# A column sum over 32768 rows: another cut of the last rows, fewer passes on the tensor engine and one sum on GpSimd

## The chip, the cores and the metric

The kernel runs on one core of a Trainium2 chip. The time is in device microseconds for one execution. A core has five engines that run side by side, each with its own queue of instructions: TensorE (PE in the profile), VectorE (DVE), ScalarE (ACT), GpSimd (POOL) and SyncE (SP), which here only starts transfers. Transfers are carried out by 16 DMA engines. Engines wait for each other and for transfers through semaphores. SBUF is the on-chip memory of 128 partitions; TensorE writes its results to PSUM, a second and smaller memory.

## The reference

The input `grad_output` has the shape 32 x 1024 x 2048 in float32, 268 MB. The result is its sum over the first two axes, 2048 numbers:

```python
def reference(grad_output):
    return np.sum(grad_output, axis=(0, 1)).astype(np.float32)
```

## The kernel before

The input is read as 32768 rows of D = 2048 columns. A *row* below means 128 of these, one on each of the 128 partitions: 1 MB, and there are 256. Everything lies in three buffers of SBUF, `ring[0]` to `ring[2]`, each with room for M = 8 rows. `load(s, at, m)` (line 53) starts one transfer on SP's queue, which brings the next m rows into buffer s from place `at` on. `plus(s, to, n, s2, of)` (line 60) is one VectorE instruction, which adds n rows of buffer s2 to n rows of buffer s. `fold(s, m, left)` (line 64) halves m rows by such sums until `left` remain. All of them run in the order in which they are written, each engine's in its own queue; a wait is set only where one needs what another engine wrote or where a place is still being read.

**The chain** (lines 90 to 99) takes 29 loads of 8 rows. Of each load the first four rows take up the running four rows of the buffer before, and then the last four rows are added: two sums of 4 x 2048 columns for 8 rows. At the end four rows of a running sum stand in the last buffer, here called `run`.

**The end** (lines 102 to 143) covers the remaining 24 rows. They come as 8 rows in `s8`, 7 in `s7`, 3 in `run` at places 4 to 6, 3 in `run` at places 1 to 3, and three last rows that come singly, each cut in two: the first C = 1792 columns and, after all three, the last B = 256 columns (`LATE`). VectorE folds `run`'s four running rows to one (place 0), `s8`'s eight to one, `s7`'s seven to two, and adds `run`'s place 5 to its place 4. The three last rows go to places of `s8` that its sums no longer need: places 1 to 3, and 4 for the 256-column ends. SP's queue holds the loads in the order of the program, so a load that waits holds up those behind it.

**TensorE** adds up the partitions. `sums(s, at)` (line 76), called a row pass here, multiplies a column of ones with one row. It has four matmuls, each of a quarter of the columns, which work beside each other in four column groups of the array and add their results into partitions 0, 32, 64 and 96 of `acc` in PSUM. A float32 matmul stands in the profile as two records, so a pass has 8 records of matmuls and 8 of weight loads. There are twelve passes in a fixed order: `run` 6, `run` 0, `s8` 0, `s7` 0, `s7` 1, `run` 1, 2, 3, `s8` 1, `s8` 2, `run` 4, `s8` 3 (the number is the place in the buffer). After these come six small matmuls for the 256-column ends, into `accr`.

**The result** (lines 147 to 161): ScalarE copies `acc` to SBUF (`res`); ScalarE and GpSimd copy 384 columns each into `joint`; VectorE adds `accr`; three transfers write the 2048 numbers out. GpSimd's copy (line 150) is all that it computes in this kernel.

Of the kernel before, what the change touches and what calls it, by code (L numbers as in the profile page):

```python
# [1 line left out]

# [4 lines left out]

P = 128
M = 8
SLOTS = 3  # L10
CHAIN = 29
B = 256
LATE = 3


@with_exitstack
def kernel(
    ctx: ExitStack,
    tc: tile.TileContext,
    grad_output: bass.AP,  # L20
    out: bass.AP,
):

    nc = tc.nc
    f32 = mybir.dt.float32
    D = out.shape[-1]
    flat = grad_output.rearrange("b s d -> (b s) d")
    Q = D // 4
    H = B // 2
    C = D - B
    add = mybir.AluOpType.add

    sb = ctx.enter_context(tc.tile_pool(name="sb", bufs=1))
    ps = ctx.enter_context(tc.tile_pool(name="ps", bufs=1, space=bass.MemoryType.PSUM))
    ring = [sb.tile([P, M * D], f32, name=f"ring{s}") for s in range(SLOTS)]
    ones = sb.tile([P, 1], f32, name="ones")
    res = sb.tile([P, Q], f32, name="res")
    joint = sb.tile([P, C - 2 * Q], f32, name="joint")
    acc = ps.tile([P, 512], f32, name="acc")
    accr = ps.tile([P, 512], f32, name="accr")
    q, v, t, a, p = nc.sync, nc.vector, nc.tensor, nc.scalar, nc.gpsimd

    row = 0

    def load(s, at, m):

        nonlocal row
        src = flat[row * P : (row + m) * P].rearrange("(p m) d -> p (m d)", p=P)
        q.dma_start(out=ring[s][:, at * D : (at + m) * D], in_=src)
        row += m

    def plus(s, to, n, s2, of):  # L60
        part = ring[s][:, to * D : (to + n) * D]
        v.tensor_tensor(out=part, in0=part, in1=ring[s2][:, of * D : (of + n) * D], op=add)  # L62

    def fold(s, m, left):
        while m > left:
            n = m // 2
            plus(s, 0, n, s, m - n)
            m -= n

    def shares(x):  # L70


        ends = x[:, 2 * Q :].rearrange("p (b g c) -> p g b c", g=2, c=H)
        return [x[:, :Q], x[:, Q : 2 * Q], ends[:, 0], ends[:, 1]]

    def sums(s, at, w=D):
        for g, x in enumerate(shares(ring[s][:, at * D : at * D + w])):
            o = acc[32 * g : 32 * g + 1, : Q if g < 2 else (w - 2 * Q) // 2]
            t.matmul(  # L79
                o if g < 2 else o.rearrange("p (b c) -> p b c", c=H),  # L80
                lhsT=ones[:],
                rhs=x,
                start=False,
                stop=False,
                tile_position=(0, 32 * g),
                skip_group_check=True,
            )

    with tc.manual_schedule():
        for i in range(CHAIN):  # L90
            s = i % SLOTS
            load(s, 0, M)
            if i == 0:
                v.memset(ones[:], 1.0)  # L94
                v.memset(acc[:], 0.0)  # L95
                v.memset(accr[:], 0.0)  # L96
            else:
                plus(s, 0, 4, (i - 1) % SLOTS, 0)
            plus(s, 0, 4, s, 4)


        run, s8, s7 = (s, *((s + k) % SLOTS for k in (1, 2)))
        load(s8, 0, 8)
        fold(run, 4, 1)
        load(s7, 0, 7)
        fold(s8, 8, 1)
        load(run, 4, 3)
        fold(s7, 7, 2)
        plus(run, 4, 1, run, 5)
        load(run, 1, 3)  # L110
        tail = flat[row * P :]
        for k in range(3):
            q.dma_start(
                out=ring[s8][:, (1 + k) * D : (1 + k) * D + C], in_=tail[k * P : (k + 1) * P, :C]
            )
        for k in range(LATE):
            q.dma_start(
                out=ring[s8][:, 4 * D + k * B : 4 * D + (k + 1) * B],
                in_=tail[k * P : (k + 1) * P, C:],
            )  # L120
        sums(run, 6)
        sums(run, 0)
        sums(s8, 0)
        sums(s7, 0)
        sums(s7, 1)
        for at in (1, 2, 3):
            sums(run, at)
        sums(s8, 1, C)
        sums(s8, 2, C)
        sums(run, 4)  # L130
        sums(s8, 3, C)
        for k in range(LATE):
            for g in (2, 3):
                x = 4 * D + k * B + (g - 2) * H
                t.matmul(  # L135
                    accr[32 * g : 32 * g + 1, :H],
                    lhsT=ones[:],
                    rhs=ring[s8][:, x : x + H],
                    start=False,
                    stop=False,  # L140
                    tile_position=(0, 32 * g),
                    skip_group_check=True,
                )

        a.copy(out=res[0:97, :], in_=acc[0:97, :])  # L147
        left = joint[64:65, :].rearrange("p (b g c) -> p g b c", g=2, c=H)
        for g, copy in enumerate((a.copy, p.tensor_copy)):
            copy(  # L150
                out=left[:, g],
                in_=res[64 + 32 * g : 65 + 32 * g, : Q - H].rearrange("p (b c) -> p b c", c=H),
            )
        v.tensor_tensor(  # L154
            out=res[64:97, Q - H :], in0=res[64:97, Q - H :], in1=accr[64:97, :H], op=add
        )
        q.dma_start(out=out[: 2 * Q].rearrange("(g c) -> g c", g=2), in_=res[0:33:32, :])
        a.dma_start(out=out[None, 2 * Q : C], in_=joint[64:65, :])
        q.dma_start(
            out=out[C:].rearrange("(g c) -> g c", g=2), in_=res[64:97:32, Q - H :]  # L160
        )
# [1 line left out]
_INS = ['grad_output']  # L163
_OUTS = [((2048,), 'float32')]


# [23 lines left out]
```

## Time and profile before

| what | value |
|---|---|
| median of three runs | 631.58 us (629.75 to 631.66) |
| the profiled execution | 630.45 us |
| span of its instructions | 628.7 us |
| read from HBM | 268.44 MB, 427 GB/s over the span |
| VectorE busy | 85% of the span, 69 instructions |
| TensorE, ScalarE, GpSimd busy | 2%, 0%, 0% |

A profile is one execution. Its times are counted from the first instruction; "busy" leaves out waits, and what stands in brackets with an arrow behind an instruction is how long its engine was idle before it and which engine or transfer ended that. The kernel moves the whole input once, and all its sums lie beside the transfers. Only what follows the last transfers is not covered by them. A line of the profile is the line of the kernel that made the instruction; since `plus` makes all of VectorE's sums, they all have line 62 and are told apart by their sizes: 8192 columns for four rows, 6144 for three, 4096 for two, 2048 for one. The share and the rate of transfers in short windows go up and down with where the packets end; over some ten microseconds they are exact.

### The profile page before, as it was taken

The numbers are of one execution on the slowest core, as the hardware profiler recorded it, in microseconds if no ns is written. First come the engines' busy times: TensorE is split into PE (matmuls) and PEld (weight loads), VectorE is DVE, ScalarE is ACT, GpSimd is POOL, SyncE is SP. The second block draws the span as 40 slices with busy tenths as digits, with TensorE's granted clock in tenths as the row PEclk, the third lists the DMA queues.
The fourth block names the chain that finished last, engine by engine and source line by source line (L and its number), as shares of the span: only waits on it lengthen the run. The fifth ranks groups of instructions, "written<-read, shape, count | busy, mean of one in ns | idle before, by whom it ended". The sixth has DMA issues, their size and how long they took to land.

```text
span 628.7 us, 443 instructions
## 1 busy us (share of the span) xinstructions
PE 13.5 (2%) x108; PEld 3.1 (0%) x108; DVE 531.9 (85%) x69; ACT 2.4 (0%) x3; POOL 0.7 (0%) x5
## 2 busy tenths in 40 slices
PE   0000000000000000000000000000000000000026
PEld 0000000000000000000000000000000000000001
DVE  0538988889888899888898888988889988889993
ACT  0000000000000000000000000000000000000000
POOL 0000000000000000000000000000000000000000
PEclk9999999999999999999999999999999999999999
DMA  9999999999999999999999999999999999999996
GB/s 400 404 463 400 467 400 467 400 467 400 467 400 467 400 467 400 467 400 467 400 467 400 467 400 467 401 463 404 463 404 463 404 463 404 459 409 459 413 411 254
DMA packets 5629, 268.48 MB, mean 427 GB/s; under 512 B 629, under 2 KB 1015, under 8 KB 1402
## 3 DMA queue, kind: packets, MB, share of 16 engines
q1 hardware_dynamic: 5624, 268.44, 99.0%
q8 instruction: 1, 0.02, 0.0%
q14 instruction: 2, 0.02, 0.0%
q10 hardware_dynamic: 2, 0.00, 0.0%
HBM read 268.44 MB, written 0.01 MB: 427 GB/s over the span
## 4 chain that ended last, share of the span: by engine, by line
issue 99%; POOLq 0%
POOLq L185 0%; POOLq L174 0%
## 5 line engine op out<-in xcount | busy, mean ns | idle before, releaser
L62 DVE TENSOR_TENSOR ring<-ring 128x8192 f32<-128x8192 f32 (+3 forms) x37 | 287.2, 7769 | 21.8 <-DMA ring<-in_grad_output_dram 20.7
L62 DVE TENSOR_TENSOR ring<-ring,ring 128x8192 f32<-128x8192 f32 x28 | 243.4, 8693 | 64.2 <-DMA ring<-in_grad_output_dram 64.2
L79 PE MATMUL acc<-ring,ones 128*1 128x512 f32 (+1 forms) x96 | 13.1, 688 | 611.3 <-DMA ring<-in_grad_output_dram 609.5
L154 DVE TENSOR_TENSOR res<-res,accr 33x128 f32<-33x128 f32 x1 | 0.3, 293 | 6.4 <-ACT res L147 6.4
L79 PEld LDWEIGHTS acc<-ring,ones 128*1 128x1 f32 x96 | 2.6, 90 | 620.8 <-issue 615.6
L147 ACT COPY res<-acc 97x512 f32<-97x512 f32 x1 | 0.6, 587 | 621.6 <-PE acc L79 621.6
L147 ACT ACT_TABLE_LOAD x1 | 1.3, 1283 | 1.5 <-DVE acc L95 1.5
L150 POOL COPY joint<-res 1x384 f32<-1x384 f32 x1 | 0.5, 502 | 624.6 <-ACT res L147 624.6
L135 PE MATMUL accr<-ring,ones 128*1 128x128 f32 x12 | 0.8, 272 | 0.0
L94 DVE MEMSET ones<- 128x1 f32 x1 | 0.1, 59 | 0.8 <-PEq L174 0.8
L95 DVE MEMSET acc<- 128x512 f32 x1 | 0.5, 485 | 0.1
L135 PEld LDWEIGHTS accr<-ring,ones 128*1 128x1 f32 x12 | 0.5, 84 | 0.5 <-DMA ring<-in_grad_output_dram 0.2
L96 DVE MEMSET accr<- 128x512 f32 x1 | 0.5, 485 | 0.1
L150 ACT COPY joint<-res 1x384 f32<-1x384 f32 x1 | 0.5, 507 | 0.0
L174 POOL MEMSET const-bfloat16-1.0<- 128x1 bf16 x1 | 0.1, 102 | 0.0
L174 POOL MEMSET const-uint8-127<- 128x1 uint8 x1 | 0.1, 100 | 0.0
L174 POOL MEMSET const-float32-0.0<- 128x1 f32 x1 | 0.1, 99 | 0.2 <-issue 0.2
L174 POOL MEMSET const-float32-1.0<- 128x1 f32 x1 | 0.1, 99 | 0.0
## 6 DMA issues: line engine op xcount, KB each, us to landing
ring<-in_grad_output_dram SPq DMA_DIRECT2D x1, 7168.0 KB, 27.5
ring<-in_grad_output_dram SPq DMA_DIRECT2D x2, 3072.0 KB
ring<-in_grad_output_dram SPq DMA_DIRECT2D x3, 896.0 KB, 16.1
ring<-in_grad_output_dram SPq DMA_DIRECT2D x30, 29.9
ring<-in_grad_output_dram SPq DMA_DIRECT2D x3, 128.0 KB, 16.6
out_dram<-res SPq DMA_DIRECT2D x1, 4.0 KB
out_dram<-joint ACTq DMA_DIRECT2D x1, 3.0 KB
out_dram<-res SPq DMA_DIRECT2D x1, 1.0 KB
```

What stands on the lines that cost most here:

```text
L62: v.tensor_tensor(out=part, in0=part, in1=ring[s2][:, of * D : (of + n) * D], op=add)
L79: t.matmul(o if g < 2 else o.rearrange("p (b c) -> p b c", c=H), lhsT=ones[:], rhs=x, start=False, stop=False, tile_position=(0, 32 * g), ...
L94: v.memset(ones[:], 1.0)
L95: v.memset(acc[:], 0.0)
L96: v.memset(accr[:], 0.0)
L135: t.matmul(accr[32 * g : 32 * g + 1, :H], lhsT=ones[:], rhs=ring[s8][:, x : x + H], start=False, stop=False, tile_position=(0, 32 * g), sk ...
L147: a.copy(out=res[0:97, :], in_=acc[0:97, :])
L150: copy(out=left[:, g], in_=res[64 + 32 * g : 65 + 32 * g, : Q - H].rearrange("p (b c) -> p b c", c=H),)
L154: v.tensor_tensor(out=res[64:97, Q - H :], in0=res[64:97, Q - H :], in1=accr[64:97, :H], op=add)
L174: nc = _bacc.Bacc("TRN2", target_bir_lowering=False, num_devices=1)
```

## The change

The 24 rows of the end are cut as 8, 7, 4 and 2 rows and the three single ones. `s8`'s eight rows are folded by VectorE to two, and the sum of these two is made by GpSimd (`plus` takes the engine as an argument). `s7`'s seven rows are folded to one, not two. `run` takes four rows at places 4 to 7, of which VectorE adds 5 and 6 to 4, and two rows at places 1 and 2. The last three rows go to places 2 to 4 of `s8` and their ends to place 5. There are ten row passes: `run` 7, `run` 0, `s8` 0, `s7` 0, `run` 1, `run` 2, `s8` 2, `s8` 3, `run` 4, `s8` 4.

```diff
-    def plus(s, to, n, s2, of):
+    def plus(s, to, n, s2, of, engine=nc.vector):
         part = ring[s][:, to * D : (to + n) * D]
-        v.tensor_tensor(out=part, in0=part, in1=ring[s2][:, of * D : (of + n) * D], op=add)
+        engine.tensor_tensor(
+            out=part, in0=part, in1=ring[s2][:, of * D : (of + n) * D], op=add
+        )
...
         load(s7, 0, 7)
-        fold(s8, 8, 1)
-        load(run, 4, 3)
-        fold(s7, 7, 2)
+        fold(s8, 8, 2)
+        plus(s8, 0, 1, s8, 1, p)
+        load(run, 4, 4)
+        fold(s7, 7, 1)
         plus(run, 4, 1, run, 5)
-        load(run, 1, 3)
+        plus(run, 4, 1, run, 6)
+        load(run, 1, 2)
         tail = flat[row * P :]
         for k in range(3):
             q.dma_start(
-                out=ring[s8][:, (1 + k) * D : (1 + k) * D + C], in_=tail[k * P : (k + 1) * P, :C]
+                out=ring[s8][:, (2 + k) * D : (2 + k) * D + C], in_=tail[k * P : (k + 1) * P, :C]
             )
         for k in range(LATE):
             q.dma_start(
-                out=ring[s8][:, 4 * D + k * B : 4 * D + (k + 1) * B],
+                out=ring[s8][:, 5 * D + k * B : 5 * D + (k + 1) * B],
                 in_=tail[k * P : (k + 1) * P, C:],
             )
-        sums(run, 6)
+        sums(run, 7)
         sums(run, 0)
         sums(s8, 0)
         sums(s7, 0)
-        sums(s7, 1)
-        for at in (1, 2, 3):
-            sums(run, at)
-        sums(s8, 1, C)
+        sums(run, 1)
+        sums(run, 2)
         sums(s8, 2, C)
+        sums(s8, 3, C)
         sums(run, 4)
-        sums(s8, 3, C)
+        sums(s8, 4, C)
```

The small matmuls at the end read place 5 in place of 4 (`x = 5 * D + ...`).

## The prediction

> **What bounds the kernel now.** I read the head of the profile page and its queues first, to see which resource is full over the whole span.
>
> ```profile
> span 628.7 us, 443 instructions
> ...
> PE 13.5 (2%) x108; PEld 3.1 (0%) x108; DVE 531.9 (85%) x69; ACT 2.4 (0%) x3; POOL 0.7 (0%) x5
> ...
> q1 hardware_dynamic: 5624, 268.44, 99.0%
> ```
>
> SP's input queue is busy 99% of the span: the transfers bound the kernel, VectorE (85%) is second, TensorE and GpSimd hardly work. So the change can only matter where the stream ends. I read that stretch by windows (columns: length, busy time and count of each engine, granted clock, DMA share, GB/s).
>
> ```profile
> 609.40:614.65 5.25, 5.16 (x24) 0.73 (x24) 5.21 (x2) 0.00 (x0) 0.00 (x0) 1.00 1.05 449
> 616.41:623.28 6.87, 6.86 (x64) 1.76 (x64) 2.16 (x1) 0.00 (x0) 0.00 (x0) 1.00 0.96 383
> 623.28:625.00 1.72, 1.49 (x22) 0.65 (x20) 0.00 (x0) 0.59 (x1) 0.00 (x0) 1.00 0.02 7
> ```
>
> The DMA share falls to 0.02 at 623.28: the input ends there. A row pass of TensorE (one call of `sums`) has 8 matmul records, so the first window is 3 passes in 5.16 us, 1.72 each, and the second 8 passes in 6.86 us, 0.86 each, at the same granted clock of 1.00. Then the timeline of the end, for what waits on what.
>
> ```profile
> 605.46 1.28 SPq L113 DMA_DIRECT2D ring<-in_grad_output_dram  x3
> ...
> 609.47 5.16 PE L79 MATMUL acc<-ring,ones 128*1 128x512 f32 x24 [609.47 <-DMA ring<-in_grad_output_dram]
> ...
> 616.42 7.89 PE L79 MATMUL acc<-ring,ones 128*1 128x512 f32 x72 [1.78 <-DVE ring L62]
> ...
> 623.28 0.10 PEld L79 LDWEIGHTS acc<-ring,ones 128*1 128x1 f32 x8 [0.77 <-DMA ring<-in_grad_output_dram]
> ...
> 624.39 0.59 ACT L147 COPY res<-acc 97x512 f32<-97x512 f32 x1 [621.57 <-PE acc L79]
> ```
>
> TensorE works without a break from 616.42. Its ninth pass there could start at 616.42 + 8 x 0.857 = 623.28 by its own backlog, and its data (third tail row) lands at 606.3 + 16.9 = 623.2 by the issue view. So TensorE's backlog and the stream end together, within 0.1 us. ScalarE's copy at 624.39 and the rest follow from that pass at fixed distance. Last, VectorE's single rows and the forms:
>
> ```profile
> 598.68 4.42 DVE L62 TENSOR_TENSOR ring<-ring 128x4096 f32<-128x4096 f32 x1
> 605.35 6.55 DVE L62 TENSOR_TENSOR ring<-ring 128x6144 f32<-128x6144 f32 x1
> 611.94 4.42 DVE L62 TENSOR_TENSOR ring<-ring 128x4096 f32<-128x4096 f32 x1
> 616.28 2.29 DVE L62 TENSOR_TENSOR ring<-ring 128x2048 f32<-128x2048 f32 x1
> ```
>
> ```profile
> L62 DVE TENSOR_TENSOR ring<-ring 128x2048 f32<-128x2048 f32 x3 | 6.9, 2290 | 0.1
> L150 ACT COPY joint<-res 1x384 f32<-1x384 f32 x1 | 0.5, 507 | 0.0
> L150 POOL COPY joint<-res 1x384 f32<-1x384 f32 x1 | 0.5, 502 | 624.6 <-ACT res L147 624.6
> L154 DVE TENSOR_TENSOR res<-res,accr 33x128 f32<-33x128 f32 x1 | 0.3, 293 | 6.4 <-ACT res L147 6.4
> ```
>
> VectorE is back to back from 565.84 to 618.57; its idle there is 0.1 us.
>
> **The change part by part.** *Transfers.* The same 268.44 MB in as many issues; 3 + 3 rows become 4 + 2. The first three landed between 602.06 (`s7`'s load, 574.56 + 27.5) and TensorE's start on them at 609.47, 2.47 us each, so four land at 602.06 + 9.9 = 611.9 and the two after them where the three did, near 616.7. SP's tail issues now wait for the second sum of `s8` (598.68 + 4.42 = 603.1), not the third (605.4); they are 2.3 us earlier but stand behind about 12 us of queued data, so nothing lands earlier. Packets of 32 and 16 KB for 24 KB have no row: 57 KB ones (`s7`, between 555.21 + 29.9 = 585.1 and 602.06) took 2.42 us a row and 24 KB ones 2.47, so I take 0 and bound it by +-0.1 us. The end of the stream stays 623.28.
>
> *TensorE* loses two passes at 0.857: 1.71 us of backlog. What is late next is the last landing, at once, so of the 1.71 nothing shortens the profiled execution. The first pass moves from 609.47 to 611.9.
>
> *VectorE* loses the third sum of `s8` (2.29) and gains the last of `s7` and one of `run` (2 x 2.29): net +2.29. If nobody disturbs it: `s7` starts at 603.03 (now 605.35 with a 0.08 us overlap, less one sum), 6.55 to 609.58; 4.42 with a 0.03 us gap to 614.04; 2.29 to 616.36; two `run` sums to 618.57 and 620.89. So `s7` row 0 is ready for TensorE at 616.4 (as before), `run` row 4 at 620.94 (was 618.6). Then TensorE: `run` 7 at 611.9, `run` 0, `s8` 0 at 1.72 to 617.1; `s7` 0, slow at worst, to 618.8; `run` 1, `run` 2, `s8` 2, `s8` 3 at 0.857 to 622.2; `run` 4 to 623.1; `s8` 4 at 623.28, when its row lands. `run` row 4 is needed by 623.28 - 0.857 = 622.43, so VectorE has 1.5 us to spare. That spare is all the cover of this step.
>
> *GpSimd* gains one sum of 2048 columns with two inputs; no such operation is in the trace. From below: not faster than VectorE's 2.29 us. From above: its copy of 384 columns took 0.502 us, its fixed part included; scaled to 2048 columns that is 2.68, and twice, for two inputs, 5.35. I take 4.0, the middle of the copy's 2.68 and 5.35. A page of the Trainium skill, GPSIMD Engine Reference, section Performance versus the Vector engine, gives 4.5 us for this very sum; the forecast by it would be 0.5 us later.
>
> *Who waits for it.* `s8` row 0, TensorE's third pass at 615.3, with all later passes behind it in order; on GpSimd's own queue only its copy of line 150 stands behind. Alone, 603.1 + 4.0 = 607.1 is early enough by 8 us. But VectorE is never idle from 603.0 to 620.9, and its sums read two SBUF operands, as GpSimd's does. No row shows two such sums side by side: the only pair, GpSimd's copy at 625.04 beside VectorE's 0.29 us sum (one input in PSUM), shows the copy no longer than ScalarE's (502 against 507 ns), which says nothing for two SBUF inputs. Bounds: side by side free (0), or one at a time.
>
> One at a time, `s7`'s first sum (no dependence on the sum before it) has begun at 603.03 before GpSimd is released at 603.1. GpSimd waits for it until 609.58, works in VectorE's 0.03 us gap before the dependent next sum, and VectorE goes on 4.0 later. Then `s8` 0 is ready at 613.6, in time; `s7` 0 at 620.4, `run` 4 at 624.94. TensorE idles 617.1 to 620.4, does five passes to 624.7, `run` 4 to 625.8, and `s8` 4 starts at 625.8 instead of 623.28: +2.5 us. The tail behind it is unchanged. I take this: with a cover of 1.5 us any real sharing of the operands' path decides, and the one free pair is the far row.
>
> The Trainium skill says the same of it on SBUF — State Buffer, section Who interferes with whom: a VectorE instruction with two SBUF inputs contends with a GpSimd instruction that reads SBUF, and the later one is held until the first is done. No run here shows it yet. By it the sum is the one just worked; without it, the rival below.
>
> **Sum.** Transfers 0, fewer passes 0, two more sums behind cover 0, GpSimd's turn 4.0 less 1.5 of cover: +2.5. The profiled execution took 630.45 us (span 628.7 and 1.75 around it): 633.0. The median of the runs shown is 631.58, 1.1 above it; nothing in the profile says that this excess goes, so the forecast is 631.58 + 2.5 = 634.1. Ends: GpSimd 2.29 gives +0.8; 5.35 gives +3.9, and if TensorE is slow again after its 3.3 us pause, +6.2 (`s7` 0 at 621.8, three passes at 1.72, three at 0.857, `s8` 4 at 629.5). On profile and median, 631.3 to 637.8. With 4.0 and slow passes: 620.4 + 3 x 1.72 + 3 x 0.857 = 628.1, +4.9. The nearest pause in the trace, 1.78 us, was followed by fast passes, so I take fast ones. TensorE: Matmul & The Clock Gate, Part 1, of the Trainium skill has the array go back to half rate after about 3.4 us of idleness, close to this pause; that would be the slow case.
>
> **Rivals.** *Side by side, not slower.* Place: the two sums between 603 and 609. For it: the free pair at 625. Then the last landing sets the end: 630.45 by the profile. TensorE gets 0.2 to 1 us of room it lacks now; if the runs at 631.6 are late because its passes stayed slow past 616.4, they lose up to 1.7 us, so 629.7 to 631.6. It decides as long as sharing costs VectorE under 1.5 us. Against: it needs sharing that is nearly free, and only a pair of another kind shows that.
>
> *GpSimd never gets a turn.* VectorE's gaps are 0.03 us, less than the 0.06 us from ScalarE's end to GpSimd's start at 625.04. GpSimd then sums from 620.9 to 624.9. TensorE stands before `s8` 0 from 615.3 to 624.9, then three passes at 1.72 and four at 0.857 put `s8` 4 at 633.5: +10.2, 640.7 (638.1 with fast passes, 642.0 with 5.35). Against: a request that waits is there before VectorE's next.
>
> *Other*: a transfer that starts late because of an unseen wait of SP.
>
> **How the numbers follow.** Taking turns 0.55 (fast 0.33, slow 0.22), side by side 0.27, no turn 0.13, other 0.05. 0.3% (1.9 us) is about what a measurement of this kernel tells from no change. Turns with a short GpSimd sum stay within it (0.12), the rest (0.43), no turn and part of other are slower: 0.60. Side by side is 0.15 the same, 0.12 faster; part of other is 0.01 the same. Same 0.28, faster 0.12. The range runs from side by side's 629.7 to 638.0, the top of taking turns, and leaves out no turn and other.
>
> **What would show it.** Right: a VectorE sum near 609.6 to 616 that starts some 4 us late, or is that much longer than its form's mean; GpSimd's sum ending near 613.6; TensorE waiting for VectorE near 620 and again for `run` row 4; ScalarE's copy near 626.9. Wrong: VectorE's sums back to back to 620.9 and TensorE's last wait on a DMA (side by side); TensorE's third pass waiting for GpSimd past 616 (no turn); the last row landing off 623.2 (transfers).

## The result, and the profile after

The changed kernel takes 634.84 us (median of five runs, 634.09 to 636.14) against 631.58 before (also five runs, 629.75 to 631.66): 1.0059 times as long, with a 95% interval of 1.0041 to 1.0077. The forecast was 634.1, in a range of 629.7 to 638.0, slower. The profiled execution took 634.56 us with a span of 632.8, 4.1 more than before.

These are the groups of VectorE's shorter sums and of GpSimd's in the changed kernel (count, then busy time and the mean duration in ns):

```profile
L62 DVE TENSOR_TENSOR ring<-ring 128x4096 f32<-128x4096 f32 x3 | 17.5, 5819 | 0.1
L62 POOL TENSOR_TENSOR ring<-ring 128x2048 f32<-128x2048 f32 x1 | 10.8, 10752 | 602.7 <-DVE ring L62 602.7
L62 DVE TENSOR_TENSOR ring<-ring 128x2048 f32<-128x2048 f32 x4 | 9.1, 2290 | 0.1
L62 DVE TENSOR_TENSOR ring<-ring 128x6144 f32<-128x6144 f32 x1 | 6.6, 6551 | 0.0
```

Only one form has changed its duration: the 4096-column sums, from a mean of 4425 ns to 5819. One of the three has done that alone. The timeline of the changed kernel shows which one (start, length):

```profile
602.98 6.55 DVE L62 TENSOR_TENSOR ring<-ring 128x6144 f32<-128x6144 f32 x1
603.14 10.75 POOL L62 TENSOR_TENSOR ring<-ring 128x2048 f32<-128x2048 f32 x1 [602.70 <-DVE ring L62]
...
609.56 8.61 DVE L62 TENSOR_TENSOR ring<-ring 128x4096 f32<-128x4096 f32 x1
618.21 2.29 DVE L62 TENSOR_TENSOR ring<-ring 128x2048 f32<-128x2048 f32 x1
620.42 2.28 DVE L62 TENSOR_TENSOR ring<-ring 128x2048 f32<-128x2048 f32 x1
622.74 2.29 DVE L62 TENSOR_TENSOR ring<-ring 128x2048 f32<-128x2048 f32 x1
```

The first sum of 4096 columns in `s7`, 4.42 us before, lasts 8.61. GpSimd's sum is given as 10.75 us long, but VectorE's 6144-column sum before it was running until 609.53 (602.98 + 6.55), and GpSimd's ended at 613.89. It worked for 4.36 us and waited for the rest; meanwhile VectorE's next sum had been issued and stood still. Neither record says that it waits: both are "busy". Then TensorE and its clock, by windows of the changed kernel (length, busy time and count of PE, PEld, DVE, ACT, POOL, then the granted clock, DMA share and GB/s), with ScalarE's copy of the result:

```profile
611.80:617.20 5.40, 5.30 (x24) 0.73 (x24) 5.40 (x1) 0.00 (x0) 2.09 (x1) 1.00 0.98 412
617.20:620.50 3.30, 0.00 (x0) 0.00 (x0) 3.27 (x3) 0.00 (x0) 0.00 (x0) 1.00 1.01 419
621.10:624.40 3.30, 3.30 (x24) 0.56 (x16) 3.27 (x2) 0.00 (x0) 0.00 (x0) 0.50 0.52 187
624.50:627.80 3.30, 3.30 (x42) 1.20 (x34) 0.53 (x1) 0.00 (x0) 0.00 (x0) 1.00 0.00 0
...
628.51 0.59 ACT L150 COPY res<-acc 97x512 f32<-97x512 f32 x1 [625.68 <-PE accr L138]
```

TensorE does three passes and stands still for 3.4 us until `s7` row 0 is ready. From 621.0 on, 0.5 us into its next passes, its granted clock is 0.50 for 3.4 us. The input ended as before (the third tail row, issued at 603.9, landed 19.3 us later, at 623.2), but TensorE has work until 628.4. ScalarE's copy starts at 628.51, 4.12 us later than before (624.39), which is the whole difference of the spans.

### The profile page after: what moved, and what is told of

It reads as the page before. It is cut to its first block, busy times and chain, and to the rows that moved or that the text cites. A ratio compares the mean times of both kernels' runs of the same rounds, so it can differ in the third digit from the quotient of the medians.

```text
span 632.8 us, 417 instructions
## 1 busy us (share of the span) xinstructions
PE 13.2 (2%) x92; PEld 3.1 (0%) x92; DVE 538.4 (85%) x70; ACT 2.4 (0%) x3; POOL 11.5 (2%) x6
## 4 chain that ended last, share of the span: by engine, by line
DMA 68%; DVE 29%; PE 1%; another core or an unknown queue 0%; issue 0%; ACT 0%; POOLq 0%; SPq 0%; DVEq 0%
DMA ring<-in_grad_output_dram 68%; DVE ring L62 29%; PE acc L81 1%; ACT res L150 0%; POOLq L188 0%; PE accr L138 0%; SPq L57 0%; DVEq L62 0%; POOLq L153 0%
## 5 line engine op out<-in xcount | busy, mean ns | idle before, releaser
L62 DVE TENSOR_TENSOR ring<-ring 128x8192 f32<-128x8192 f32 (+3 forms) x38 | 293.7, 7735 | 21.8 <-DMA ring<-in_grad_output_dram 20.7
L62 POOL TENSOR_TENSOR ring<-ring 128x2048 f32<-128x2048 f32 x1 | 10.8, 10752 | 602.7 <-DVE ring L62 602.7
```

Source lines behind the costliest of these rows:

```text
L62: engine.tensor_tensor(out=part, in0=part, in1=ring[s2][:, of * D : (of + n) * D], op=add)
```

## The experiments

Three readings were to be told apart. *Taking turns*: a sum with two SBUF inputs on VectorE and one on GpSimd do not run together, and VectorE is held for the length of GpSimd's. *The cut*: one sum more on VectorE and a later start of TensorE cost the time, and GpSimd is harmless. *The clock*: how much of the 4.1 us is TensorE's half speed. The start of a span differs by up to 0.8 us between traces, so times of two traces are compared from the landing of the third tail row, 623.2 in both traces above.

**GpSimd's sum given back to VectorE.** In the changed kernel:

```diff
-        plus(s8, 0, 1, s8, 1, p)
+        plus(s8, 0, 1, s8, 1)
```

> The changed kernel with the pair of s8 summed by VectorE instead of GpSimd; cut and ten passes unchanged. Taking turns (VectorE is held while GpSimd's sum reads): VectorE pays its own 2.29 us and nothing else, every sum lasts as its form did before, the 4096-column sum of s7 4.42 us and not 8.61. s7 row 0 ready near 616.4 + 2.3 = 618.7, run row 4 near 623.2, ScalarE's copy near 625.3 (0.9 later than in the kernel before, 3.2 earlier than in the changed one); profiled time near 631.3. Rival, the new cut is what costs (first pass later, two more sums): no better than the changed kernel, 634 to 635.

Measured: 631.91 us median of ten (630.85 to 632.89), 1.001 of before (1.000 to 1.002). The profiled execution took 632.6. The form rows and the clock of this kernel:

```profile
L62 DVE TENSOR_TENSOR ring<-ring 128x4096 f32<-128x4096 f32 x3 | 13.3, 4424 | 0.1
L62 DVE TENSOR_TENSOR ring<-ring 128x2048 f32<-128x2048 f32 x5 | 11.4, 2291 | 0.1
...
614.20:617.60 3.40, 1.17 (x12) 0.10 (x4) 3.37 (x2) 0.00 (x0) 0.00 (x0) 1.00 0.97 401
617.70:621.00 3.30, 3.04 (x16) 0.55 (x20) 3.27 (x3) 0.00 (x0) 0.00 (x0) 0.50 1.00 413
```

All sums last as before, and 2.9 us of the median are gone. So GpSimd's sum cost more than the VectorE sum that it replaced. The trace is 1.3 us later than expected (632.6 against 631.3), since here too TensorE paused and got the half clock (the five runs with a granted clock of 0.996 over their span took 631.79 to 632.89, the five with 0.999 or 1.000 took 630.85 to 632.04); the cut itself leaves such a pause when `s7` comes later than TensorE's first three passes end.

**GpSimd's sum alone, in the old cut.** The kernel before, twelve passes; only the third sum of `s8` moves:

```diff
-        fold(s8, 8, 1)
+        fold(s8, 8, 2)
+        plus(s8, 0, 1, s8, 1, p)
```

(the tail rows go one place further in `s8`, as in the change, so that they need not wait for GpSimd).

> The kernel before with its cut and twelve passes, only the third sum of s8 moved to GpSimd. Taking turns: the 4096-column sum of s7 is held to about 8.6 us, s7 rows ready near 618.2 instead of 616.4 although VectorE has one sum less, eight passes of 0.857 behind it, ScalarE's copy near 626.2, 1.8 us later than before; profiled time near 632.3, up to 634 with slow passes. Rival, the new cut is what costs and GpSimd works beside VectorE: s7 ready near 614.1, the last landing decides, 630.4.

Measured: 634.75 us in its one run. The sum of `s7` is held again:

```profile
609.30 8.62 DVE L62 TENSOR_TENSOR ring<-ring 128x4096 f32<-128x4096 f32 x1
...
613.30:616.70 3.40, 1.04 (x8) 0.10 (x8) 3.40 (x1) 0.00 (x0) 0.34 (x1) 1.00 0.87 367
616.80:623.50 6.70, 5.53 (x28) 0.98 (x32) 3.32 (x2) 0.00 (x0) 0.00 (x0) 0.50 0.87 345
```

The hold does not need the new cut, and this kernel with nothing else changed is as slow as the whole change. The time lies 0.75 above the upper end that I gave, because TensorE stood twice (0.93 us for GpSimd, 3.25 for VectorE) and the half clock lasted 6.8 us, not 3.4.

**No sum of the pair at all: two passes.** In the changed kernel, TensorE takes both rows (eleven passes):

```diff
-        plus(s8, 0, 1, s8, 1, p)
...
         sums(s8, 0)
+        sums(s8, 1)
         sums(s7, 0)
```

> The changed kernel without GpSimd's sum: TensorE takes both rows of s8, eleven passes. Taking turns: VectorE is back to back to 620.9, s7 row 0 ready at 616.4; TensorE goes without a pause from 611.85, the extra pass ends near 618, six passes of 0.857 bring the last one to about 623.3, where its row lands: profiled time near 630.5, ScalarE's copy at 624.4, as in the kernel before. Rival, the new cut costs: 633 or more.

Measured: 630.06 us median of ten (629.84 to 630.39), 0.9975 of before (0.9966 to 0.9985). This version beats both kernels. Its sums and TensorE's stretch:

```profile
L62 DVE TENSOR_TENSOR ring<-ring 128x4096 f32<-128x4096 f32 x3 | 13.3, 4424 | 0.1
...
611.40:622.80 11.40, 11.05 (x80) 2.14 (x80) 8.92 (x4) 0.00 (x0) 0.00 (x0) 1.00 0.95 390
...
623.91 0.59 ACT L150 COPY res<-acc 97x512 f32<-97x512 f32 x1 [621.09 <-PE acc L81]
```

TensorE is busy without a pause until it waits 0.35 us for the last landing; the clock stays at 1.00 and ScalarE's copy comes at once behind the input's end. The extra pass does not cost anything, it keeps TensorE at work until `s7` is ready. The cut with its extra VectorE sum is free here, as the forecast's undisturbed schedule had it.

**The pause filled.** The changed kernel with GpSimd's sum, and three more passes over a row that is there (`run` 7), into a PSUM tile that nobody reads, ahead of `sums(s7, 0)`:

```diff
+        for _ in range(3):
+            for g, x in enumerate(shares(ring[run][:, 7 * D : 8 * D])):
+                o = idle[32 * g : 32 * g + 1, :Q]
+                t.matmul(
+                    o if g < 2 else o.rearrange("p (b c) -> p b c", c=H),
+                    lhsT=ones[:],
+                    rhs=x,
+                    start=True,
+                    stop=True,
+                    tile_position=(0, 32 * g),
+                    skip_group_check=True,
+                )
         sums(s7, 0)
```

> The changed kernel with three extra row passes into an unused PSUM tile between s8 row 0 and s7 row 0, where TensorE stood idle for 3.4 us. The hold and the clock as two terms: VectorE's 4096-column sum stays at 8.6 us and s7 row 0 comes at 620.5 as before, but the granted clock stays at 1.00 from 621 to 624.4, the last pass starts at 625.9 instead of 627.4, ScalarE's copy at 627.05: 1.5 us less than the changed kernel, near 633.1 where it had 634.6. Rival, the clock's fall to 0.50 hung on nothing that TensorE did: no gain.

Measured: 632.85 us median of ten; eight runs of 632.42 to 633.11 and two at 634.3 and 634.4. In the trace VectorE is held as in the changed kernel, and the clock no longer falls:

```profile
609.08 8.62 DVE L63 TENSOR_TENSOR ring<-ring 128x4096 f32<-128x4096 f32 x1
...
616.20:620.00 3.80, 2.76 (x28) 0.47 (x20) 3.77 (x3) 0.00 (x0) 0.00 (x0) 1.00 1.02 421
620.10:626.00 5.90, 5.83 (x56) 1.47 (x58) 4.41 (x2) 0.00 (x0) 0.00 (x0) 1.00 0.39 144
626.57 0.59 ACT L163 COPY res<-acc 97x512 f32<-97x512 f32 x1 [623.74 <-PE acc L82]
```

So the two terms come apart: 2.0 us of the median (1.9 of the profiled executions) are the clock, and the hold leaves 1.3 to before's median, 2.8 to the earlier of the two groups of runs that the next experiment tells of (630.05). The two late runs have a granted clock of 0.996 over their span, the eight others 0.999 or 1.000: they lost clock after all, but no trace shows where.

**The old kernel's pause filled.** The kernel before has a pause of TensorE too (1.78 us), and its runs lie in two groups: of the 25 beside the first experiments, eight between 629.7 and 630.4 and 17 between 631.2 and 632.2. The granted clock over the span is 0.999 or 1.000 in the eight and 0.997 in all of the 17. The edit is the same, with one extra pass over `run` 6.

> The kernel before with one extra row pass into an unused PSUM tile between s8 row 0 and s7 row 0, so that TensorE has no pause of 1.8 us there. The kernel before has run in two groups, near 630.1 (8 of 25) and near 631.6 (17 of 25). Slow passes after the pause make the later group: with the pause filled all runs lie in the first, median near 630.1, like the recut with two passes (630.06), so that the new cut itself is worth nothing. Rival, the later group comes from the transfers: the two groups stay, median near 631.5.

Measured: 630.05 us median of ten, 629.74 to 630.33, 0.9988 of before (0.9978 to 0.9998; five of the 13 runs of before in that session were above 631). The later group is gone. In the one trace the pause is still 1.76 us, since the extra pass was over at 614.4; what the pass adds is busy time ahead of the pause:

```profile
613.39 1.03 PE L128 MATMUL idle<-ring,ones 128*1 128x512 f32 x8
616.19 7.89 PE L80 MATMUL acc<-ring,ones 128*1 128x512 f32 x72 [1.76 <-DVE ring L63]
...
612.44:615.85 3.41, 1.99 (x20) 0.28 (x12) 3.41 (x1) 0.00 (x0) 0.00 (x0) 1.00 0.85 361
```

The clock rose to full speed at 612.44, and in the 3.41 us from there TensorE was busy for 1.99. Without the extra pass it would have been 1.13 and the pause 2.62 (the pass before it ended at 613.57), an estimate; that is as little busy time as in the traces whose clock then fell (the table in the last section). That the pass works by this is worked out from one trace, not shown. By its time the recut with two passes (630.06) is not better than this: the new cut itself is worth nothing that shows, and what there is to gain is had by one useless pass.

Then the kernel before itself, unchanged, for a trace of each group.

> The kernel before, unchanged, for a trace of its later group (above 631). If slow passes make that group, a trace near 631.6 shows a granted clock of 0.50 for some 3.4 us after 616.4 or passes of 1.7 us there, the last landing at 623.2 as ever, and ScalarE's copy near 625.5 to 626; a trace near 630.1 shows passes of 0.86 from 616.4 on. Rival, transfers: in a late trace the last landing itself is later by more than 1 us.

> The same kernel once more, since one trace falls into either group: the same expectations.

The first came out at 631.79, the second at 630.04. The same stretch in both, and ScalarE's copy; the later run first:

```profile
609.00:616.00 7.00, 4.67 (x24) 0.72 (x24) 6.97 (x3) 0.00 (x0) 0.00 (x0) 1.00 0.97 415
616.50:619.80 3.30, 3.30 (x20) 0.67 (x16) 1.72 (x1) 0.00 (x0) 0.00 (x0) 0.50 1.01 419
619.90:625.00 5.10, 5.10 (x58) 1.70 (x54) 0.00 (x0) 0.00 (x0) 0.00 (x0) 1.00 0.52 194
625.74 0.59 ACT L147 COPY res<-acc 97x512 f32<-97x512 f32 x1 [622.92 <-PE accr L135]
```

```profile
609.00:616.00 7.00, 5.30 (x24) 0.73 (x25) 6.97 (x3) 0.00 (x0) 0.00 (x0) 1.00 0.97 415
616.50:619.80 3.30, 3.30 (x36) 0.77 (x32) 1.65 (x1) 0.00 (x0) 0.00 (x0) 1.00 1.01 419
623.99 0.58 ACT L147 COPY res<-acc 97x512 f32<-97x512 f32 x1 [621.17 <-PE acc L79]
```

The last tail row landed at 606.0 + 16.9 = 622.9 in the one and 605.9 + 16.9 = 622.8 in the other. The transfers are the same; the later run had the half clock for one stretch of 3.4 us, 20 matmuls instead of 36 in it, and its end is 1.75 us later.

**What exactly collides.** Three kernels change what GpSimd does in that place of the changed kernel. First its sum in two halves:

```diff
-        plus(s8, 0, 1, s8, 1, p)
+        for x in (0, D // 2):
+            part = ring[s8][:, x : x + D // 2]
+            p.tensor_tensor(out=part, in0=part, in1=ring[s8][:, D + x : D + x + D // 2], op=add)
```

> The changed kernel with GpSimd's sum cut in two of 1024 columns. The engines take turns instruction by instruction: the first half ends some 2.2 us after VectorE's 6144-column sum, the second not before VectorE's 4096-column sum is over; two VectorE sums are held by about 2.1 us each (4096: 6.6, the next 2048: 4.4), and s7 row 0 comes at about the time of the changed kernel (620.5). Rival, GpSimd keeps the operands' path until its queue is empty: one sum held by 4.2 to 4.4, as in the changed kernel.

Measured: 632.2 us.

```profile
602.23 6.55 DVE L62 TENSOR_TENSOR ring<-ring 128x6144 f32<-128x6144 f32 x1
602.39 8.59 POOL L111 TENSOR_TENSOR ring<-ring 128x1024 f32<-128x1024 f32 x1 [601.95 <-DVE ring L62]
608.81 6.44 DVE L62 TENSOR_TENSOR ring<-ring 128x4096 f32<-128x4096 f32 x1
610.94 6.52 POOL L111 TENSOR_TENSOR ring<-ring 128x1024 f32<-128x1024 f32 x1
615.29 4.31 DVE L62 TENSOR_TENSOR ring<-ring 128x2048 f32<-128x2048 f32 x1
```

They alternate, one instruction each. The first half ends 2.20 us after VectorE's 6144-column sum (610.98 against 608.78); the 4096-column sum is held by 2.02 us; the second half ends at 617.46, 2.20 after that sum's end at 615.26, and now the 2048-column sum is held by 2.02. VectorE loses 4.04 us in all, as much as in one piece (4.19). Here `s8` row 0 kept TensorE at work at 617.5, and the clock did not fall; hence 632.2.

Then a copy of one row for the sum of two (`p.tensor_copy` of row 1 of `s8` into row 0), and a `p.memset` of row 1. Both leave one of the two rows out of the result.

> The changed kernel with GpSimd copying a row of 2048 columns (one input) where it added two; the sum of row 1 of s8 into row 0 is left out. If what holds VectorE is that GpSimd reads SBUF at all, the 4096-column sum is held for as long as the copy lasts: 2.7 us by the 384-column copy's rate, less if that one was mostly fixed cost; it lasts 6.1 to 7.1 us. If the hold needs two inputs on both sides, it lasts its own 4.42.

> The changed kernel with GpSimd writing zeros to row 1 of s8 (2048 columns, no input) where it added it to row 0; that sum is left out. If the reading is what collides, VectorE's 4096-column sum lasts its own 4.42 us, all its sums are back to back to 620.9 and the time is that of the recut with two passes, near 630.1 (less one pass, which has no effect). If any GpSimd work in SBUF collides, the sum is held.

The copy first:

```profile
602.35 8.15 POOL L109 COPY ring<-ring 128x2048 f32<-128x2048 f32 x1 [601.91 <-DVE ring L62]
...
608.79 5.99 DVE L62 TENSOR_TENSOR ring<-ring 128x4096 f32<-128x4096 f32 x1
```

Then the memset:

```profile
602.53 1.80 POOL L109 MEMSET ring<- 128x2048 f32 x1 [602.09 <-DVE ring L62]
...
608.98 4.42 DVE L62 TENSOR_TENSOR ring<-ring 128x4096 f32<-128x4096 f32 x1
```

The copy waited for VectorE's 6144-column sum as the sum did, ended 1.75 us after it (610.50 against 608.75) and held VectorE's next by 1.57 us, a bit less than I gave (5.99 against 6.1 to 7.1: more of the 384-column copy was fixed cost). The memset ran for 1.80 us in the middle of the 6144-column sum and held nothing. In these traces what collides is GpSimd reading SBUF; one input is enough. Times were 629.83 and 630.05, so a hold of 1.57 us still fits into the cover.

## Why the prediction was right, and where it was not

- *Taking turns* was right in place, order and cause: GpSimd released behind an independent sum that had begun, let in when that sum ended at 609.53 (609.58 forecast), in VectorE's gap of 0.03 us, one VectorE sum held. The rule of the Trainium skill (SBUF — State Buffer, Who interferes with whom) agrees with the traces: 4.19 us of hold against a sum, 1.57 against a copy, none against a memset, the last as the page has it for instructions that only write.
- *The price* of GpSimd's sum, 4.0 us by rows, was 4.36 of work and 4.19 of hold. The 4.5 us that the Trainium skill states for this sum (GPSIMD Engine Reference, Performance versus the Vector engine) are nearer.
- *The cover* of 1.5 us was right: VectorE ended `run` row 4 at 625.03, and TensorE could have taken it 0.05 us later (as it took `s7` row 0, ended at 620.50, at 620.55); with full speed behind it the last pass would have started at 625.94, 2.66 after 623.28 (2.5 forecast). The copy experiment, whose hold is about as long as the cover, ended no later than the kernel before.
- *Fast passes after the pause* was the step that failed. I took the pause of 1.78 us as the nearest row to one of 3.3 and so full speed; the clock fell. The two pauses were not alike: in the 3.41 us after the clock's rise TensorE was busy for 1.63 us in the kernel before and for 0.48 in the changed one (last section). Three passes took 4.27 us instead of 2.57, and TensorE came to `run` row 4 at 626.1 when that had been ready since 625.08. So the end did not hang on `run` row 4, as I had it, but on `s7` row 0 and the slow backlog behind it. The last pass (its 512-column parts) started at 627.40 and not at 625.94: 1.46 us. ScalarE's copy came at 628.51, not near 626.9. The slow case stood in the text with a chance of 0.22. The same wrong reading is in "at the same granted clock of 1.00": the first three passes of the kernel before, 1.72 us each, lie ahead of the first entry in the trace's list of clocks, and that entry (614.37) is their rise to full speed.
- *The sum came out right by an exchange, which is luck.* On the profile it was 633.0 against 634.56 measured: 0.16 missing in the hold and 1.46 in the clock, less rounding. The 1.1 us that I added because the runs shown lie above their profile were just such a loss by the clock in the kernel before. I had named that as a possibility in the rival alone; the two traces of the kernel before show it.
- *Transfers, fewer passes, later first load: 0* held. The two-pass version ends with the input, and is not faster than the old cut with its pause filled.
- The rivals: GpSimd had its turn at the first gap, so the case of no turn did not come; working side by side was seen, but only with a memset.

## What to carry to other kernels

Handing a sum to GpSimd while VectorE runs sums with two SBUF inputs did not take work off VectorE here: it was held for GpSimd's whole instruction, 4.2 us for a sum that it does itself in 2.3. In the profile this showed only as an instruction that lasts longer than its form's mean on the one engine and starts its record early on the other; so compare means by form before and after. Where TensorE's last backlog ends together with the last landing, a short pause ahead of it can halve its clock in some runs and not in others: look for two groups of times, and keep it busy with useful or useless passes until the data are there.

## What the runs showed of the hardware

TensorE's clock fell after a pause of 2.3 us in the late run of the kernel before; after 1.78 us, in its profiled execution, it stayed at 1.00. Each trace has a list of granted clocks. It begins with the rise to full speed, 3.1 to 5.8 us after TensorE's first pass began; ahead of it nothing is listed and the windows above read 1.00, although passes there take 1.72 us and later ones 0.86. From the rise on the clock keeps one value for 3.41 us or a whole multiple of it, until the trace ends (616.45 to 619.86 at 0.50 in the late run, 6.83 us at 0.50 in the old cut with GpSimd's sum). What came next went with how long TensorE was busy in the first 3.41 us after the rise:

| trace | clock rose at | busy in the next 3.41 us | clock then |
|---|---|---|---|
| changed kernel | 617.62 | 0.48 | 0.50 |
| GpSimd's sum in the old cut | 613.29 | 1.04 | 0.50 |
| kernel before, late run | 613.03 | 1.16 | 0.50 |
| sum given back to VectorE | 614.18 | 1.19 | 0.50 |
| sum in two halves | 614.60 | 1.46 | 1.00 |
| kernel before, profiled | 614.37 | 1.63 | 1.00 |
| copy | 614.31 | 1.66 | 1.00 |
| kernel before, early run | 614.31 | 1.77 | 1.00 |
| old kernel's pause filled | 612.44 | 1.99 | 1.00 |
| changed kernel's pause filled | 615.99 | 2.97 | 1.00 |
| memset | 614.53 | 3.24 | 1.00 |
| two passes | 615.94 | 3.41 | 1.00 |

In these twelve traces the limit lies between 1.19 and 1.46 us of 3.41. The length of the longest pause sorts them as well (2.26 us or more in the four, 1.95 or less in the others); but each fall came 3.41 us after the rise, and between 1.97 us (GpSimd's sum in the old cut) and 3.88 us (changed kernel) after the pause's start. One program falls on either side of it, as the rise comes earlier or later in its first passes: 613.03 and 614.31 in the two runs of the kernel before.

The Trainium skill (TensorE: Matmul & The Clock Gate, Part 1) has such windows of 3.4 us that run freely, which agrees, and lets the array go cold after an idle window. The traces differ in that the window before the fall need not be idle: TensorE was busy for 1.19 of 3.41 us ahead of it in the kernel with VectorE's sum, and for 1.04 of 3.41 in the old cut with GpSimd's.
